# A decoder trunk in float32r: h as contiguous rows of 512 values at one byte offset from the weights

## The chip, the cores and the metric

The kernel runs on one core of one Trainium2 chip. The metric is the device time of one execution in microseconds (us). The time before is 2643.68 us, the median of three runs (2642.72 to 2644.52).

The engines are named as in the profile: PE is TensorE (matmuls), PEld its weight loads, DVE VectorE, ACT ScalarE, POOL GpSimd, SP SyncE. SBUF is the on-chip memory with 128 partitions, PSUM the memory of eight banks that matmuls write. A matmul holds a block of 128 x 128 weights, the stationary operand, which a weight load puts in place beforehand, and streams the moving operand past it, up to 512 values per partition. Offsets in this text are bytes within a partition.

## The reference, cut to what matters

The reference is a trunk of two layers for one sequence of 256 tokens with a width of 2048. Layer 0 has a retention mixer of eight heads, layer 1 a short gated convolution. Each is followed by a SwiGLU feed-forward part with an inner width of 5632. Ahead of each of these four parts stands a normalization with a shift and a scale that come from a conditioning vector c:

```python
for i in range(DEPTH):
    mod = (c_act @ w_mod[i] + b_mod[i])[:, None, :]
    sh1, sc1, g1, sh2, sc2, g2 = jnp.split(mod, 6, axis=-1)
    h = (rms_norm(x, norm1_g[i]) * (1.0 + sc1) + sh1).astype(x.dtype)
    ...
    x = (x + g1 * y).astype(x.dtype)
    h = (rms_norm(x, norm2_g[i]) * (1.0 + sc2) + sh2).astype(x.dtype)
    x = (x + g2 * swiglu(h, ffn_w_in[i], ffn_w_out[i])).astype(x.dtype)
return rms_norm(x, final_g).astype(x.dtype)
```

Most of the work lies in the products of activations with float32 weight matrices: `ret_w_in`, `ret_w_out`, `ffn_w_in` and `ffn_w_out` (twice), `conv_w_in` and `conv_w_out`. In the retention mixer q and k are rotated by `rope`:

```python
t1, t2 = t[..., :half], t[..., half:]
return jnp.concatenate([t1 * cos - t2 * sin, t2 * cos + t1 * sin], axis=-1)
```

## The kernel before, in words

**Layout.** The model width lies on the partitions: x and every activation are kept as 16 tiles (index j or k) of 128 rows by 256 tokens. A product with a weight matrix goes over k, and for each k over the columns of a group of weight columns (class `Group`).

**Two halves.** The matmuls take the type float32r, which holds fewer bits than float32. So every number is split in a high half, the value rounded to float32r, and a low half, the remainder. A product of two split numbers is made of three parts: high by high, high weights by low activations, low weights by high activations. An activation tile has the shape [128, 2, 256], high half first.

**Weights.** All weights lie in one array in the order of use. `fetch` loads chunks of 128 x 2048 float32 by DMA from SP's queue. `prepare` (from L297) splits half a chunk, 1024 columns, into a tile hi (ScalarE, L312) and a tile lo (VectorE, L315). The pool `wpool` has four tiles each of hi and lo, of 4096 bytes per partition. `take` (L320) hands out the next 128 columns of hi and lo, so blocks of weights stand 512 bytes apart in these tiles.

**Products.** There are four ways, all on TensorE, whose order is as written in the program:

- `product` (from L347) makes a pair of matmuls for each block: L357 streams all 512 values of the activation tile, both halves, past the high weights; L360 streams the 256 values of the high half past the low weights.
- `packed` (from L376) makes three matmuls of 256 values, L397 to L399, which add up in 256 columns of a bank.
- `by_token` (from L367) makes the values of the retention. It holds blocks of h (128 tokens of one half) as weights and streams hi and lo, 512 columns each: L372 to L374, once for each half of the tokens.
- `normed` (from L493) makes the first columns of the stage behind a normalization: six columns (`LEAD`), while the root of the norm is still unknown. h is then only x times its scale (`scaled_only`, L484). For every k all the columns of the group follow one another (L516 to L518). The row of h has two tokens more than 256 here: the shift, split in a high and a low part, so that the product with the shift comes out in columns of its own. `total` (L529) multiplies the sum by the root and adds the product with the shift (`end`).

**Activation operands.** These are `h_all` in the pool `hpool` (L481), 16 tiles with two halves of 256 + 2 values each, so that the halves of one tile stand 258 values apart; `rm` tiles (from L567), the retention's middle; and `mid` tiles (from L939), the middle of the feed-forward part and of the convolution. rm and mid tiles are contiguous rows of 512 values. The pools are declared in the order `const`, `work`, `wpool`, `hpool`, then `rm` and `rpool`, or `mpool` after these are closed.

**Order of stages.** The retention's input goes first: four spans over some heads and some k, then head by head in a fixed order (`projections`, L915), with the first half of its output product (`ret_out`) after four heads and the second after eight. The feed-forward part runs in two halves of 22 tiles, each followed by its output product. The convolution follows, and the second feed-forward part. `rope` (L804) rotates q and k of a head on VectorE: one product of 512 values with the cosine, two of 256 with the sine, and two of 256 to add them up. Its input lies in PSUM, or, for heads whose product was begun in the spans, in an SBUF tile (`pair`, L899). Between the products the modulations of the next stages are made (`modulation`, L241), as VectorE products with the spread vector c; `paced` (L269) says when.

Of the kernel before, what the change touches and what calls it, by code (L numbers as in the profile page):

```python
# [10 lines left out]
F32 = mybir.dt.float32  # L11
F32R = mybir.dt.float32r
I32 = mybir.dt.int32
AF = mybir.ActivationFunctionType
ALU = mybir.AluOpType
PSUM = bass.MemoryType.PSUM

P = 128
D = 2048
S = 256  # L20
KT = D // P
# [27 lines left out]
STEPS = (8, 8, 20)  # L49
RAW_BUFS = 3  # L50
PART_BUFS = 4

Q0, K0, V0, G0 = 0, HEADS * DK, 2 * HEADS * DK, 2 * HEADS * DK + HEADS * DV
SH1, SC1, GT1, SH2, SC2, GT2 = range(6)
# [133 lines left out]
def trunk(ctx: ExitStack, tc: tile.TileContext, x_in, c_in, pos_in, w_mod, cols_in, tab_in, w_all, out):  # L188
    nc = tc.nc
    const = ctx.enter_context(tc.tile_pool(name="const", bufs=1))  # L190
    work = ctx.enter_context(tc.tile_pool(name="work", bufs=2))
    wpool = ctx.enter_context(tc.tile_pool(name="wpool", bufs=PART_BUFS))
    ps = ctx.enter_context(tc.tile_pool(name="ps", bufs=8, space=PSUM))
# [3 lines left out]
    def name(s):  # L197
        serial[0] += 1
        return f"{s}_{serial[0]}"

    def tmp(tag, shape=(P, S), dtype=F32, pool=work, bufs=None):
        return pool.tile(list(shape), dtype, tag=tag, name=name(tag), bufs=bufs)
# [30 lines left out]
    mod_s = [[const.tile([P, KT], F32, tag=f"s{l}{i}", name=f"s{l}{i}") for i in range(2)] for l in range(DEPTH)]  # L233
# [35 lines left out]
    def paced(n):  # L269

        units[0] += n
        due = 0
        for (a, i), (b, j) in zip(plan_mod, plan_mod[1:]):
            if units[0] >= a:
                due = min(j, i + (units[0] - a) * (j - i) // (b - a))
        allowed[0] = min(allowed[0] + n * MOST, 2.0) if n <= 64 else 0.0
        while todo and n_mod - len(todo) < due and allowed[0] >= 1.0:
            allowed[0] -= 1.0
            modulation(*todo.pop())

    def needed(layer, which, last=KT - 1):
        while any(m[:2] == (layer, which) and m[2] <= last for m in todo):
            modulation(*todo.pop())
# [36 lines left out]
    def take(group, k, col, width=P):  # L320

        assert order.pop() == (group, k, col, width)
        i = taken_cols[0] % HALF
        if i == 0:
            if ready and taken_cols[0]:
                ready.pop(0)
            while len(ready) < 1 + AHEAD * (units[0] >= first):
                n = len(ready)
                prepare()
                if len(ready) == n:  # L330
                    break
        taken_cols[0] += width
        return [t[:, i : i + width] for t in ready[0]]

    def bank():
        return ps.tile([P, 2, S], F32, tag="bank", name=name("bank"))
# [91 lines left out]
    def norm_sums(accs):  # L428

        pt = bank()  # L430
        for t in range(2):
            for i, acc in enumerate(accs):
                nc.tensor.matmul(
                    pt[:, 0, t : t + 1], acc[:, t * P : (t + 1) * P], ones[:, 0:1],
                    start=i == 0, stop=i == len(accs) - 1,
                )
        return pt

    def norm_roots(pt, n):
        return roots_of(pt[:, 0, 0:2], n)  # L440
# [9 lines left out]
    def norm_spread(r):  # L450

        pb = bank()
        for t in range(2):
            nc.tensor.matmul(
                pb[:, 0, t * P : (t + 1) * P], r[:, t : t + 1].to_broadcast([P, P]), ident, start=True, stop=True
            )
        return pb[:, 0, :]
# [18 lines left out]
    def modulated(h, j, rb, layer, norm):  # L476
        shifted(h, scaled(j, rb, layer, norm), j, layer, norm)

    hpool = ctx.enter_context(tc.tile_pool(name="hpool", bufs=1))

    h_all = hpool.tile([P, KT, 2, S + 2], F32R, tag="h", name="h")  # L481
    h = [h_all[:, j, :, :S] for j in range(KT)]

    def scaled_only(layer, norm, j):  # L484

# [7 lines left out]
    def normed(accs, layer, norm, g):  # L493

        needed(layer, SH2 if norm else SH1)
        shift = mod_s[layer][norm].unsqueeze(2).to_broadcast([P, KT, 2])  # L500
        ends = [h_all[:, :, i, S:] for i in range(2)]
        nc.scalar.copy(ends[0], shift)
        nc.vector.tensor_tensor(ends[1], shift, ends[0].bitcast(F32), op=ALU.subtract)
        banks = [bank().rearrange("p a b -> p (a b)")[:, : S + 2] for _ in g.cols]
        made = [0]

        def more(n):
            while made[0] < n:
                modulated(h[made[0]], made[0], root, layer, norm)
                made[0] += 1  # L510

        for k in g.ks:
            rows = [h_all[:, k, i, :] for i in range(2)]
            for c, pt in zip(g.cols, banks):
                hi, lo = take(g, k, c)
                nc.tensor.matmul(pt, hi, rows[0], start=k == 0, stop=False)  # L516
                nc.tensor.matmul(pt, hi, rows[1], start=False, stop=False)  # L517
                nc.tensor.matmul(pt, lo, rows[0], start=False, stop=k == KT - 1)  # L518
            if k == ROOTS_AT:
                r = norm_roots(norm_sums(accs), D)  # L520
            elif k == SPREAD_AT:
                root = tmp("rb", bufs=1)
                nc.scalar.copy(root, norm_spread(r))
            elif k > SPREAD_AT:
                more(min(k, made[0] + 2))
        more(KT)
        paced(len(g.cols) * len(g.ks))

        def total(pt, dst=None):  # L529
            end = tmp("end", (P, 1), bufs=2)  # L530
            nc.scalar.copy(end, pt[:, S : S + 1])
            t = tmp("low", bufs=3)
            nc.vector.tensor_tensor(t, pt[:, :S], root, op=ALU.mult)
            dst = tmp("sum", bufs=4) if dst is None else dst
            nc.scalar.activation(dst, t, AF.Identity, bias=end)
            return dst

        return [lambda dst=None, pt=pt: total(pt, dst) for pt in banks]

    def output(groups, act, which, last, after=None, base=None):  # L540
# [25 lines left out]
    with ExitStack() as inner:  # L566
# [46 lines left out]
        sin = rm.tile([P, S], F32, tag="sin", name="sin")  # L613
        cos = rm.tile([P, S], F32, tag="cos", name="cos")
        ahead = {}
# [15 lines left out]
        with tc.tile_pool(name="start", bufs=1) as sp:  # L631
# [59 lines left out]
            with tc.manual_schedule(engines={mybir.EngineType.DVE, mybir.EngineType.Activation}):  # L691
# [16 lines left out]
                for i in range(0, D, 2 * S):  # L708
                    pt = bank().rearrange("p a b -> p (a b)")
# [24 lines left out]
                pt = norm_sums([acc[0][:, 0, :]])  # L734
# [66 lines left out]

        rp = inner.enter_context(tc.tile_pool(name="rpool", bufs=1))

        def rope(s, tag):  # L804
            a = tmp("qa", (P, 2, S), pool=rp, bufs=1)
            nc.vector.tensor_tensor(a, s, cos.unsqueeze(1).to_broadcast([P, 2, S]), op=ALU.mult)
            b = tmp("qb", (P, 2, S), pool=rp, bufs=1)
            nc.vector.tensor_tensor(b[:, 0, :], s[:, 1, :], sin, op=ALU.mult)
            nc.vector.tensor_tensor(b[:, 1, :], s[:, 0, :], sin, op=ALU.mult)
            nc.vector.tensor_tensor(a[:, 0, :], a[:, 0, :], b[:, 0, :], op=ALU.subtract)  # L810
            nc.vector.tensor_tensor(a[:, 1, :], a[:, 1, :], b[:, 1, :], op=ALU.add)
            dst = rp.tile([P, 2, 2, S], F32R, tag=tag, name=name(tag))
            nc.scalar.copy(dst[:, 0, :, :], a)
            nc.vector.tensor_tensor(dst[:, 1, :, :], a, dst[:, 0, :, :].bitcast(F32), op=ALU.subtract)
            return dst

        def gate(s):

            g = rp.tile([P, 2, S], F32, tag="sg", name=name("sg"), bufs=2)
            nc.scalar.activation(g, s, AF.Silu)  # L820
            return g.rearrange("p a b -> p (a b)")
# [77 lines left out]
        def pair(head, i):  # L899

            g = RET_HEADS[head][0][i]
            if not g.ks:
                return [ahead[head, n] for n in ((i,) if i < 2 else (2, 3))]
            sums = packed(g, h)
            for j, pt in enumerate(sums):
                key = (head, i + j)
                if key in tag_of:
                    free.append(tag_of.pop(key))
                if key in ahead:
                    s = tmp("qs", (P, 2, S), pool=rp, bufs=1)  # L910
                    nc.vector.tensor_tensor(s, ahead[key], pt, op=ALU.add)
                    sums[j] = s
            return sums

        def projections(head):  # L915
            q = rope(*pair(head, 0), "q")
            k = rope(*pair(head, 1), "k")
            v = values(head, RET_HEADS[head][1])
            sp = scores(head, q, k)
            sg = [gate(s) for s in pair(head, 2)]  # L920
            asides.extend(mixed(head, sp, v, sg))
            since[0] = 0
# [48 lines left out]
    for i, g in enumerate(CONV_IN):  # L971
        pending += [sums(g)] if i else normed(acc, 1, 0, g)
        while len(pending) >= 3:
            pb, pc, pu = pending[:3]
            pending = pending[3:]
            j = done
            b, c, u = pb(tmp("bsum", pool=mpool, bufs=2)), pc(), pu()
# [73 lines left out]
```

## Time and profile before

| what | value |
|---|---|
| median of the three runs | 2643.68 us |
| the profiled execution, its own time | 2641.89 us |
| its span, from the first to the last instruction | 2640.1 us |
| mean granted TensorE clock | 0.998 |
| matmuls on PE | 15220 |
| bytes read from HBM | 682.99 MB, 259 GB/s over the span |

Pairs (L357 and L360) run in long chains, by operand and stage: with rm in windows such as 374.8 to 429.9 us and 715.7 to 774.7 us; with h such as 1169.8 to 1399.7 us; with mid such as 1402.8 to 1514.8 us.

How to read the rows that follow: a group has its line in the kernel, the engine, the operation, output <- inputs by the names of the tiles, the shape, and the count (x3296); behind the first bar stand the busy time in us and the mean of one in ns, behind the second the idle time of the engine ahead of them and what ended it. A row of a single line's view has the least, median and largest duration in ns, and the start of the first and of the last instruction in us. A row of the timeline has the start and the duration in us. Matmuls are pipelined and their ends are modelled, so durations of neighbours overlap; their starts are recorded.

### The profile page before, as it was taken

The numbers are of one execution on the slowest core, as the hardware profiler recorded it, in microseconds if no ns is written. First come the engines' busy times: TensorE is split into PE (matmuls) and PEld (weight loads), VectorE is DVE, ScalarE is ACT, GpSimd is POOL, SyncE is SP. The second block draws the span as 40 slices with busy tenths as digits, with TensorE's granted clock in tenths as the row PEclk, the third lists the DMA queues.
The fourth block names the chain that finished last, engine by engine and source line by source line (L and its number), as shares of the span: only waits on it lengthen the run. The fifth ranks groups of instructions, "written<-read, shape, count | busy, mean of one in ns | idle before, by whom it ended". The sixth has DMA issues, their size and how long they took to land.

```text
span 2640.1 us, 38225 instructions
## 1 busy us (share of the span) xinstructions
PE 2608.1 (99%) x15220; PEld 2291.2 (87%) x15220; DVE 1990.3 (75%) x2543; ACT 1244.8 (47%) x1770; POOL 146.6 (6%) x230
## 2 busy tenths in 40 slices
PE   7999999999999999999999999999999999999998
PEld 5888889888889888888888898888988888888887
DVE  7998878777698877777777888888886765555554
ACT  5644443444455444344444454444554443444443
POOL 0000001010000011110100001100000000000000
PEclk9999999999999999999999999999999999999999
DMA  9976668776686877777777768777677655555553
GB/s 397 391 273 256 258 242 317 258 271 259 251 300 243 314 283 272 273 283 283 287 270 282 268 224 321 280 281 262 253 277 263 248 219 191 190 191 187 183 190 127
DMA packets 96950, 687.58 MB, mean 260 GB/s; under 512 B 10753, under 2 KB 12545, under 8 KB 13825
## 3 DMA queue, kind: packets, MB, share of 16 engines
q1 hardware_dynamic: 96770, 685.13, 70.0%
q8 instruction: 119, 1.95, 0.3%
q14 instruction: 61, 0.50, 0.1%
HBM read 682.99 MB, written 2.10 MB: 259 GB/s over the span
## 4 chain that ended last, share of the span: by engine, by line
PE 76%; issue 19%; DVE 2%; DMA 1%; ACT 1%; POOL 0%; DVEq 0%; POOLq 0%; ACTq 0%
PE bank L357 35%; PE bank L360 18%; PE bank L372 4%; PE bank L373 4%; PE bank L374 4%; PE bank L399 2%; PE bank L398 2%; PE bank L397 2%; PE bank L517 1%; PE bank L516 1%; PE bank L518 1%; DVE raw L642 1%; DMA raw<-w_all 1%; PE bank L869 1%; DVE lo L315 1%
## 5 line engine op out<-in xcount | busy, mean ns | idle before, releaser
L315 DVE TENSOR_TENSOR lo<-raw,hi 128x1024 fp32r<-128x1024 f32 x912 | 1111.5, 1222 | 551.6 <-ACT hi L312 549.3
L312 ACT CAST hi<-raw 128x1024 fp32r<-128x1024 f32 x912 | 953.2, 1050 | 1088.9 <-PE bank L357 649.0
L357 PE MATMUL bank<-h,hi 128*128 128x512 f32 x3296 | 1155.2, 395 | 0.0
L360 PE MATMUL bank<-h,lo 128*128 128x256 f32 x3296 | 924.4, 280 | 0.0
L357 PEld LDWEIGHTS bank<-h,hi 128*128 128x128 f32 x3296 | 622.6, 189 | 145.3
L360 PEld LDWEIGHTS bank<-h,lo 128*128 128x128 f32 x3296 | 622.0, 189 | 0.0
L357 PE MATMUL bank<-mid,hi 128*128 128x512 f32 x1604 | 556.3, 393 | 0.0
L360 PE MATMUL bank<-mid,lo 128*128 128x256 f32 x1604 | 444.9, 277 | 0.6 <-DVE lo L315 0.6
L246 DVE SCALAR_TENSOR_TENSOR raw<-raw,cb 128x2048 f32<-128x2048 f32 x160 | 365.4, 2284 | 11.7 <-DMA raw<-w_mod 11.3
L357 PEld LDWEIGHTS bank<-mid,hi 128*128 128x128 f32 x1604 | 300.7, 187 | 69.4
L360 PEld LDWEIGHTS bank<-mid,lo 128*128 128x128 f32 x1604 | 301.3, 188 | 0.9 <-DVE lo L315 0.9
L372 PE MATMUL bank<-hi,h 128*128 128x512 f32 x512 | 202.7, 396 | 0.0
L373 PE MATMUL bank<-lo,h 128*128 128x512 f32 x512 | 201.9, 394 | 0.0
L374 PE MATMUL bank<-hi,h 128*128 128x512 f32 x512 | 201.9, 394 | 0.0
L357 PE MATMUL bank<-rm,hi 128*128 128x512 f32 x496 | 174.2, 396 | 0.0
L399 PE MATMUL bank<-h,lo 128*128 128x256 f32 x512 | 145.6, 284 | 9.1 <-DVE lo L315 9.1
L397 PE MATMUL bank<-h,hi 128*128 128x256 f32 x512 | 144.9, 283 | 2.5 <-ACT h L670 2.5
L398 PE MATMUL bank<-h,hi 128*128 128x256 f32 x512 | 144.8, 283 | 0.5 <-DVE h L671 0.5
L360 PE MATMUL bank<-rm,lo 128*128 128x256 f32 x496 | 138.5, 279 | 0.0
L374 PEld LDWEIGHTS bank<-hi,h 128*128 128x128 f32 x512 | 96.3, 188 | 22.7
L372 PEld LDWEIGHTS bank<-hi,h 128*128 128x128 f32 x512 | 96.6, 189 | 19.6
L373 PEld LDWEIGHTS bank<-lo,h 128*128 128x128 f32 x512 | 96.4, 188 | 19.6
(152 smaller groups left out, 2239.3 us busy)
## 6 DMA issues: line engine op xcount, KB each, us to landing
raw<-w_all SPq DMA_DIRECT2D x456, 1024.0 KB, 4.8
raw<-w_mod SPq DMA_DIRECT2D x192, 1024.0 KB, 5.0
x<-x_in SPq DMA_DIRECT2D x4, 512.0 KB, 5.7
out<-out SPq DMA_DIRECT2D x5, 256.0 KB, 3.4
decay<-tab_in SPq DMA_DIRECT2D x8, 128.0 KB, 2.2
out<-out SPq DMA_DIRECT2D x3, 128.0 KB, 2.5
out<-out SPq DMA_DIRECT2D x1, 384.0 KB, 2.7
cols<-cols_in SPq DMA_DIRECT2D x1, 160.0 KB, 8.8
```

What stands on the lines that cost most here:

```text
L246: nc.vector.scalar_tensor_tensor(raw, raw, 1.0, cb, op0=ALU.mult, op1=ALU.mult, accum_out=total)
L312: nc.scalar.copy(hi, raw)
L315: nc.vector.tensor_tensor(lo, raw, hi.bitcast(F32), op=ALU.subtract)
L357: nc.tensor.matmul(pt, hi, h, start=fresh and k == g.ks[0], stop=False, skip_group_check=True)
L360: nc.tensor.matmul(pt[:, 1, :], lo, h[:, 0, :], start=False, stop=last and k == g.ks[-1], skip_group_check=True)
L372: nc.tensor.matmul(o, ht[:, 0, :], hi, start=first, stop=False)
L373: nc.tensor.matmul(o, ht[:, 0, :], lo, start=False, stop=False)
L374: nc.tensor.matmul(o, ht[:, 1, :], hi, start=False, stop=last)
L397: nc.tensor.matmul(pt, hi, h[:, 0, :], start=first, stop=False, skip_group_check=True)
L398: nc.tensor.matmul(pt, hi, h[:, 1, :], start=False, stop=False, skip_group_check=True)
L399: nc.tensor.matmul(pt, lo, h[:, 0, :], start=False, stop=last, skip_group_check=True)
L516: nc.tensor.matmul(pt, hi, rows[0], start=k == 0, stop=False)
```

## The change

The change has three parts.

1. h's row becomes 32 values of margin and then the two halves, 256 values each, side by side: [128, 16, 32 + 512] in place of [128, 16, 2, 258]. A tile of 8 values (32 bytes per partition) that nothing uses is taken ahead of h_all in the same pool.
2. The shift's two tokens, its high and its low part, stand in the last two values of the margin, in front of the high half. In `normed` the high rows keep 258 values (two tokens and 256), the low rows have 256 and are added to columns 2 and on of the bank. Before, the high half's tokens held the shift's high part and the low half's its low part, so one column of the bank had the whole product; now its two parts come out in two columns, and `total` adds them with one small ScalarE instruction more.
3. `rope` makes both sine products in one instruction of 512 values, written over its input where that lies in SBUF (`ours`), and else to a tile under the tag qs. The tile qb is gone.

Order, groups, loads and the number of matmuls stay.

```diff
+LEFT, MARGIN = 8, 32
...
-    h_all = hpool.tile([P, KT, 2, S + 2], F32R, tag="h", name="h")
-    h = [h_all[:, j, :, :S] for j in range(KT)]
+    hpool.tile([P, LEFT], F32, tag="aside", name="aside")
+    h_all = hpool.tile([P, KT, MARGIN + 2 * S], F32R, tag="h", name="h")
+    h = [h_all[:, j, MARGIN:].rearrange("p (a b) -> p a b", a=2) for j in range(KT)]
...
-        shift = mod_s[layer][norm].unsqueeze(2).to_broadcast([P, KT, 2])
-        ends = [h_all[:, :, i, S:] for i in range(2)]
+        shift = mod_s[layer][norm].unsqueeze(2)
+        ends = [h_all[:, :, MARGIN - 2 + i : MARGIN - 1 + i] for i in range(2)]
...
-            rows = [h_all[:, k, i, :] for i in range(2)]
+            high, low = h_all[:, k, MARGIN - 2 : MARGIN + S], h[k][:, 1, :]
...
-                nc.tensor.matmul(pt, hi, rows[0], start=k == 0, stop=False)
-                nc.tensor.matmul(pt, hi, rows[1], start=False, stop=False)
-                nc.tensor.matmul(pt, lo, rows[0], start=False, stop=k == KT - 1)
+                nc.tensor.matmul(pt, hi, high, start=k == 0, stop=False, skip_group_check=True)
+                nc.tensor.matmul(pt[:, 2:], hi, low, start=False, stop=False, skip_group_check=True)
+                nc.tensor.matmul(pt, lo, high, start=False, stop=k == KT - 1, skip_group_check=True)
...
-            end = tmp("end", (P, 1), bufs=2)
-            nc.scalar.copy(end, pt[:, S : S + 1])
+            low_end = tmp("end", (P, 1), bufs=4)
+            nc.scalar.copy(low_end, pt[:, 1:2])
+            end = tmp("end", (P, 1), bufs=4)
+            nc.scalar.activation(end, pt[:, 0:1], AF.Identity, bias=low_end)
             t = tmp("low", bufs=3)
-            nc.vector.tensor_tensor(t, pt[:, :S], root, op=ALU.mult)
+            nc.vector.tensor_tensor(t, pt[:, 2:], root, op=ALU.mult)
...
-        def rope(s, tag):
+        def rope(s, tag, ours):
+
             a = tmp("qa", (P, 2, S), pool=rp, bufs=1)
             nc.vector.tensor_tensor(a, s, cos.unsqueeze(1).to_broadcast([P, 2, S]), op=ALU.mult)
-            b = tmp("qb", (P, 2, S), pool=rp, bufs=1)
-            nc.vector.tensor_tensor(b[:, 0, :], s[:, 1, :], sin, op=ALU.mult)
-            nc.vector.tensor_tensor(b[:, 1, :], s[:, 0, :], sin, op=ALU.mult)
-            nc.vector.tensor_tensor(a[:, 0, :], a[:, 0, :], b[:, 0, :], op=ALU.subtract)
-            nc.vector.tensor_tensor(a[:, 1, :], a[:, 1, :], b[:, 1, :], op=ALU.add)
+            b = s if ours else tmp("qs", (P, 2, S), pool=rp, bufs=1)
+            nc.vector.tensor_tensor(b, s, sin.unsqueeze(1).to_broadcast([P, 2, S]), op=ALU.mult)
+            nc.vector.tensor_tensor(a[:, 0, :], a[:, 0, :], b[:, 1, :], op=ALU.subtract)
+            nc.vector.tensor_tensor(a[:, 1, :], a[:, 1, :], b[:, 0, :], op=ALU.add)
...
-            q = rope(*pair(head, 0), "q")
-            k = rope(*pair(head, 1), "k")
+            q = rope(*pair(head, 0), "q", (head, 0) in ahead)
+            k = rope(*pair(head, 1), "k", (head, 1) in ahead)
```

## The prediction

> **What bounds the kernel now.** I read the first two parts of the page first, then the chain of waits.
>
> ```profile
> span 2640.1 us, 38225 instructions
> PE 2608.1 (99%) x15220; PEld 2291.2 (87%) x15220; DVE 1990.3 (75%) x2543; ACT 1244.8 (47%) x1770; POOL 146.6 (6%) x230
> ...
> PEclk9999999999999999999999999999999999999999
> ...
> PE 76%; issue 19%; DVE 2%; DMA 1%; ACT 1%; POOL 0%; DVEq 0%; POOLq 0%; ACTq 0%
> PE bank L357 35%; PE bank L360 18%; PE bank L372 4%; PE bank L373 4%; PE bank L374 4%; PE bank L399 2%; PE bank L398 2%; PE bank L397 2%; PE bank L517 1%; PE bank L516 1%; PE bank L518 1%; DVE raw L642 1%; DMA raw<-w_all 1%; PE bank L869 1%; DVE lo L315 1%
> ```
>
> TensorE is the bound: it is busy 99% of the span at the full granted clock, and the chain runs through its matmuls and their issue. So the time changes by what the pitch of the matmuls changes, that is the time from the start of one to the start of the next. The groups say how many there are of each kind:
>
> ```profile
> L357 PE MATMUL bank<-h,hi 128*128 128x512 f32 x3296 | 1155.2, 395 | 0.0
> L357 PE MATMUL bank<-mid,hi 128*128 128x512 f32 x1604 | 556.3, 393 | 0.0
> L372 PE MATMUL bank<-hi,h 128*128 128x512 f32 x512 | 202.7, 396 | 0.0
> L357 PE MATMUL bank<-rm,hi 128*128 128x512 f32 x496 | 174.2, 396 | 0.0
> ```
>
> Each L357 (512 values) is followed by one L360 (256 values); I call the two a pair. The mean of one (395 ns) is no pitch, as ends are modelled and overlap. For the pitch I took the view of line L357 alone in four windows that hold nothing but pairs, one row for each (count, durations, first and last start):
>
> ```profile
> L357 PE MATMUL bank<-h,hi x657: 389/396/400, 1169.8 to 1399.7; 128*128 128x512 f32 x165
> L357 PE MATMUL bank<-mid,hi x324: 392/394/395, 1402.8 to 1514.8; 128*128 128x512 f32 x162
> L357 PE MATMUL bank<-rm,hi x160: 392/394/395, 374.8 to 429.9; 128*128 128x512 f32 x160
> L357 PE MATMUL bank<-rm,hi x168: 395/398/403, 715.7 to 774.7; 128*128 128x512 f32 x168
> ```
>
> First to last start over the count less one: **h 229.9 / 656 = 350.5 ns a pair**, mid 112.0 / 323 = 346.7, rm 55.1 / 159 = 346.5 in the first half and 59.0 / 167 = 353.3 in the second. The four windows run the same instructions on the same shapes with no wait, and differ by 2%.
>
> **Where the rows lie.** If tiles lie one behind another in the order of the pools, every weight block starts at a multiple of 512 bytes within hi and lo (4096 bytes each), and h follows them. A row of h has 2 x 258 x 4 = 2064 bytes, 16 more than a multiple of 128, so h[k] starts 16k bytes off the weights: the offset steps through eight values as k runs. mid and rm tiles have 2048 bytes; all start at the same offset, and as 16 x 2064 is a multiple of 128 that offset is 0. So before, h sweeps and mid and rm hold 0. One sweep, in the timeline of TensorE (first rows of the pairs k = 0 to 3, 6, 7, 10, 11, and k = 0 of the next column):
>
> ```profile
> 1295.63 0.39 PE L357 MATMUL bank<-h,hi 128*128 128x512 f32 x1
> ...
> 1295.97 0.39 PE L357 MATMUL bank<-h,hi 128*128 128x512 f32 x1
> ...
> 1296.32 0.39 PE L357 MATMUL bank<-h,hi 128*128 128x512 f32 x1
> ...
> 1296.67 0.39 PE L357 MATMUL bank<-h,hi 128*128 128x512 f32 x1
> ...
> 1297.71 0.40 PE L357 MATMUL bank<-h,hi 128*128 128x512 f32 x1
> ...
> 1298.07 0.40 PE L357 MATMUL bank<-h,hi 128*128 128x512 f32 x1
> ...
> 1299.13 0.40 PE L357 MATMUL bank<-h,hi 128*128 128x512 f32 x1
> ...
> 1299.48 0.40 PE L357 MATMUL bank<-h,hi 128*128 128x512 f32 x1
> ...
> 1301.23 0.39 PE L357 MATMUL bank<-h,hi 128*128 128x512 f32 x1
> ```
>
> The pair takes 0.34 us at k = 0 and 0.36 at k = 6; the cycle of 16 takes 5.60, 350 ns a pair. The pitch does depend on the row.
>
> **The change part by part.** *Held offset.* With MARGIN a row of h has 544 x 4 = 2176 bytes, 17 x 128, and the 32-byte tile in front puts every row of h 32 bytes past a multiple of 128 from the weights; the rows behind h move along, since 16 x 2176 is a multiple of 128. So every chain will hold one offset, 32. What does a held offset cost? Three chains that hold one:
>
> ```profile
> 303.54 0.85 PE L869 MATMUL bank<-v,sp 128*128 128x512 f32 x3
> 304.22 0.28 PE L397 MATMUL bank<-h,hi 128*128 128x256 f32 x1
> ...
> 1518.70 0.28 PE L397 MATMUL bank<-mid,hi 128*128 128x256 f32 x1
> ...
> 1520.86 0.28 PE L397 MATMUL bank<-mid,hi 128*128 128x256 f32 x1
> ...
> 789.98 0.28 PE L516 MATMUL bank<-h,hi 128*128 128x258 f32 x1
> ...
> 791.42 0.28 PE L516 MATMUL bank<-h,hi 128*128 128x258 f32 x1
> ```
>
> Three matmuls of 512 at offset 0: 0.68 / 3 = 226.7 ns each. Eighteen of 256 at offset 0: 2.16 / 18 = 120.0 ns. The last two rows lie in the normed product, which stays at one k for all its columns; this is k = 2, offset 32 (low half 40), and four triples of 258 take 1.44, that is 120.0 ns a matmul. From the first two: (226.7 - 120.0) / 256 = 0.417 ns a value, and 13.3 ns a matmul on top. (16 values, 64 bytes, take 6.7 ns, and 6.7 is also what parts the two rm windows: I call it a step.) A pair then costs 768 x 0.417 + 2 x 13.3 = 346.7 ns, which is what mid takes. The held chain at 32 fits the same law (258 values: 120.9).
>
> So my value for h is 346.7, by the row it becomes most like: one contiguous row of 512 with a held offset, as mid. 3296 x (346.7 - 350.5) = **-12.5 us**. The bounds are 340 (the cheapest pair of the sweep, k = 0) and 353.3 (the dear rm window, and about what the sweep pays at k = 2, 6, 10: 0.35, 0.36, 0.35): -34.6 and +9.2 us.
>
> *mid and rm* go from held 0 to held 32: mid stays at 346.7, **0**, with bounds 340 and 353.3: -10.7 and +10.6 us (1604 pairs). The dear half of rm, 248 pairs, settles at the law: 248 x -6.6 = **-1.6 us**; bounds -3.3 and 0. The cheap half moves as mid would: 0, bounds -1.6 and +1.7.
>
> *Values by token* (L372 to L374) stream the weights past blocks of h, so they sweep too, and have not the law's 226.7:
>
> ```profile
> 290.26 0.39 PE L372 MATMUL bank<-hi,h 128*128 128x512 f32 x1
> ...
> 298.62 0.39 PE L372 MATMUL bank<-hi,h 128*128 128x512 f32 x1
> ```
>
> Twelve triples in 8.36: 232.2 ns. Held, 1536 x (226.7 - 232.2) = **-8.4 us**; bounds -18 (220, one step of 6.7 lower) and 0 (the sweep as it is).
>
> *Packed products on h* (L397 to L399) stand at about 120 already; 0, bounds +-2 us (1536 matmuls by the 1 ns that a timeline of 0.01 us does not resolve). *The shift's tokens in front* leave the high row at 258 and cut the low one to 256: 288 x 2 x 0.417 = -0.24 us.
>
> *Other engines.* rope does one sine product of 512 instead of two of 256, and total one more ScalarE copy of a column:
>
> ```profile
> L806 DVE TENSOR_TENSOR qa<-qs,cos 128x512 f32<-128x512 f32 x8 | 5.5, 683 | 0.1
> L808 DVE TENSOR_TENSOR qb<-qs,sin 128x256 f32<-128x256 f32 x8 | 3.3, 416 | 0.0
> L531 ACT COPY end<-bank 128x1 f32<-128x1 f32 x18 | 2.2, 147 | 0.0
> ```
>
> 16 x (2 x 416 - 683) = 2.4 us less on VectorE, 18 x 0.147 = 2.6 us more on ScalarE. Both lie under TensorE's pairs, and I cost them at nothing. The copies come six or five to a stage, 0.9 us, while two of the eight banks stay free for further columns of 16 pairs (5.6 us each). Without that cover it would be +2.6 us; the VectorE saving can be worth at most its 2.4. No DMA and no queue is moved.
>
> **Sum**: -12.5 - 1.6 - 8.4 - 0.2 = -22.7 us. The profiled execution took 2641.89 us, 1.8 below the median of 2643.68 and 0.8 below the lowest of the three, so a median run would come out that much higher: **2619 us** from the profiled one, 2621 from the median. I say 2620, 0.9% faster.
>
> **The rivals.** *Fewer stalls* (faster still). If 32 bytes keep weight loads and rows apart, each pair falls one step of 6.7 ns below mid's, to 340: -34.6 - 10.7 - 3.3 - 1.6 and the tokens' -8.4 give -58.6, 2583 us. For it: the sweep holds a pair of 340, so the law is no floor, and other offsets than 0 have never been held in long chains. Against: the one chain held at 32 shows 120.0, no less than at 0.
>
> *Dearer at 32* (slower). Row and weight block are read at the same time, and half a step's 64 bytes apart one may hold up the other twice instead of once; then all pairs lock at the 353.3 that rm shows: +9.2 + 10.6 + 1.7, tokens unchanged: +21.5, 2663 us. For it: in the sweep k = 2, 6, 10, all 32 off a multiple of 64, are dear. Against: there the offset has just moved, and what one pair pays may have been made by the pair before. It decides from a pair pitch of 350.9, where (with the tokens' gain) the 5396 pairs cost as much as now.
>
> *No dependence on place*, the time stays at 2642 (+-3). The sweep of 0.34 to 0.36 and the two rm windows speak against it. [...]
>
> *The front tile does not shift anything* (it is never read, and may be dropped): then all chains hold 0 and the forecast's sum stands as it is; it is no case of its own.
>
> **How the numbers follow.** Forecast 0.36, fewer stalls 0.24, dearer 0.32, no dependence 0.08. Faster by over 0.2% (5 us, about what a measurement of this kernel tells from no change): 0.60; within 0.2%: 0.08; slower: 0.32. The forecast's own range is 2610 to 2630, from tokens that gain nothing to tokens at 220. Cases of both signs hold much of the chance, so the range reaches to them: down to 2578, just under the fewer-stalls sum, up to 2664, just over the dearer one.
>
> **What would show it.** Right: the windows of h and mid both give 346.7 ns a pair with the same counts, the token triples fall from 697 to 680 ns, and the rm windows are alike. Wrong by place: h and mid together at 340 or at 353.3; by the held-offset step: h and mid apart, or an h pitch that still depends on k. A cover that fails would show TensorE idle before L357 or L360 right after a normed stage.

## The result and the profile after

The changed kernel takes 2639.5 us (median of 22 runs, 2637.41 to 2643.2), the kernel before 2643.94 us (22 runs beside them, 2641.26 to 2646.61). The ratio is 0.9985, 95% interval 0.9978 to 0.9992: 4.4 us faster, a gain that the interval tells from none, and a fifth of the 23 that were forecast.

The first parts of the page of the changed kernel, and the share of the span by engine in its chain of waits:

```profile
span 2637.7 us, 38238 instructions
PE 2604.2 (99%) x15220; PEld 2299.1 (87%) x15220; DVE 1989.0 (75%) x2527; ACT 1249.3 (47%) x1788; POOL 151.3 (6%) x230
...
PEclk9999999999999999999999999999999999999999
...
PE 75%; issue 20%; DVE 2%; DMA 2%; ACT 1%; POOL 0%; DVEq 0%; ACTq 0%; POOLq 0%
```

TensorE is still the bound, busy 99% of the span at a mean granted clock of 0.998, so the answer lies in the pitches again. The view of the one line that starts a pair, now L358 (L361 is its second half), in the same four windows of the changed kernel; the columns are count, durations in ns, first and last start in us:

```profile
L358 PE MATMUL bank<-h,hi x652: 389/392/402, 1169.9 to 1397.7; 128*128 128x512 f32 x163
L358 PE MATMUL bank<-mid,hi x319: 390/390/395, 1402.6 to 1512.9; 128*128 128x512 f32 x160
L358 PE MATMUL bank<-rm,hi x155: 389/390/391, 374.6 to 428.0; 128*128 128x512 f32 x155
L358 PE MATMUL bank<-rm,hi x162: 389/390/391, 715.9 to 771.7; 128*128 128x512 f32 x162
```

h takes 227.8 / 651 = **349.9 ns** a pair (before 350.5), mid 110.3 / 318 = 346.9, rm 53.4 / 154 = 346.8 and 55.8 / 161 = 346.6. mid stayed, rm's dear half came down as forecast, and h did not move. The timeline of TensorE in the changed kernel shows what its pairs do (first rows of pairs; between the fifth and the last lie 11 more):

```profile
1199.65 0.39 PE L358 MATMUL bank<-h,hi 128*128 128x512 f32 x1
1200.00 0.39 PE L358 MATMUL bank<-h,hi 128*128 128x512 f32 x1
1200.34 0.40 PE L358 MATMUL bank<-h,hi 128*128 128x512 f32 x1
1200.70 0.39 PE L358 MATMUL bank<-h,hi 128*128 128x512 f32 x1
1201.05 0.39 PE L358 MATMUL bank<-h,hi 128*128 128x512 f32 x1
...
1205.25 0.39 PE L358 MATMUL bank<-h,hi 128*128 128x512 f32 x1
```

The starts are 0.35, 0.34, 0.36, 0.35 apart, and this repeats every four pairs: 1.40 us for four, 5.60 for sixteen. (Taken to the nanosecond and averaged over the window, the four steps are 348, 348, 359 and 345 ns.) mid, whose rows by their sizes all lie at one offset, shows no such period: its four steps in the window above, taken the same way, are 346 to 347 ns. Rows 2176 bytes apart advance by 128 modulo 512, so they come back to the same place every four rows. That suggested where to look.

The values by token did not fall from 697 to 680 ns a triple either. Timeline of L373, changed kernel, first and last of ten triples:

```profile
292.85 0.39 PE L373 MATMUL bank<-hi,h 128*128 128x512 f32 x1
...
299.15 0.40 PE L373 MATMUL bank<-hi,h 128*128 128x512 f32 x1
```

Nine steps in 6.30 us are 700 ns a triple, 233.3 a matmul, 1.1 more than before. Two small gains that were not forecast are in the timeline of the products of 256 and 258 values, packed on mid (L398) and normed (L519), 20 and 10 triples of three matmuls apart:

```profile
1516.70 0.28 PE L398 MATMUL bank<-mid,hi 128*128 128x256 f32 x1
...
1523.70 0.28 PE L398 MATMUL bank<-mid,hi 128*128 128x256 f32 x1
```

```profile
786.03 0.28 PE L519 MATMUL bank<-h,hi 128*128 128x258 f32 x1
...
789.58 0.28 PE L519 MATMUL bank<-h,hi 128*128 128x258 f32 x1
```

A packed matmul takes 7.00 / 60 = 116.7 ns, before 120.0; a normed triple 355, before 360.

**Where the time came from**, by these rows: h 3296 x (349.9 - 350.5) = -2.0 us; rm's second half 248 x (346.6 - 353.3) = -1.7; tokens 1536 x 1.1 = +1.7; normed 288 x -5 ns = -1.4; packed on mid 60 x -10 ns = -0.6. The sum, -4.0 us, lies near the 4.4 us of the medians, but it does not account for the time in full. The rows come from two executions that lie 2.4 us apart (2641.89 and 2639.47), and the list leaves out two items of that size: the packed products on h, which went from 357.2 to 353.3 ns a triple where they follow one another (512 triples, about -2.0 us), and pauses between matmuls, about 3 us more than before. Both come from the starts of the matmuls in the two traces.

### The profile page after: what moved, and what is told of

The parts are those of the page before. It is cut to its first block, busy times and chain, and to the rows that moved or that the text cites. A ratio compares the mean times of both kernels' runs of the same rounds, so it can differ in the third digit from the quotient of the medians.

```text
span 2637.7 us, 38238 instructions
## 1 busy us (share of the span) xinstructions
PE 2604.2 (99%) x15220; PEld 2299.1 (87%) x15220; DVE 1989.0 (75%) x2527; ACT 1249.3 (47%) x1788; POOL 151.3 (6%) x230
## 4 chain that ended last, share of the span: by engine, by line
PE 75%; issue 20%; DVE 2%; DMA 2%; ACT 1%; POOL 0%; DVEq 0%; ACTq 0%; POOLq 0%
PE bank L358 34%; PE bank L361 18%; PE bank L374 4%; PE bank L375 4%; PE bank L373 4%; PE bank L400 2%; PE bank L398 2%; PE bank L399 2%; PE bank L519 1%; PE bank L521 1%; PE bank L520 1%; DMA raw<-w_mod 1%; DVE raw L647 1%; DMA raw<-w_all 1%; DVE lo L316 1%
## 5 line engine op out<-in xcount | busy, mean ns | idle before, releaser
L358 PE MATMUL bank<-h,hi 128*128 128x512 f32 x3296 | 1153.8, 394 | 0.0
L361 PE MATMUL bank<-h,lo 128*128 128x256 f32 x3296 | 926.4, 281 | 0.0
L358 PEld LDWEIGHTS bank<-h,hi 128*128 128x128 f32 x3296 | 617.9, 187 | 140.0
L361 PEld LDWEIGHTS bank<-h,lo 128*128 128x128 f32 x3296 | 624.5, 189 | 0.0
L358 PE MATMUL bank<-mid,hi 128*128 128x512 f32 x1604 | 556.3, 390 | 0.0
L361 PE MATMUL bank<-mid,lo 128*128 128x256 f32 x1604 | 452.5, 282 | 1.1 <-DVE lo L316 1.1
L358 PEld LDWEIGHTS bank<-mid,hi 128*128 128x128 f32 x1604 | 301.1, 188 | 63.0
L361 PEld LDWEIGHTS bank<-mid,lo 128*128 128x128 f32 x1604 | 303.4, 189 | 1.5 <-DVE lo L316 1.5
L374 PE MATMUL bank<-lo,h 128*128 128x512 f32 x512 | 203.3, 397 | 0.2 <-DVE lo L316 0.2
L373 PE MATMUL bank<-hi,h 128*128 128x512 f32 x512 | 203.4, 397 | 0.0
L358 PE MATMUL bank<-rm,hi 128*128 128x512 f32 x496 | 172.5, 391 | 0.0
L398 PE MATMUL bank<-h,hi 128*128 128x256 f32 x512 | 144.7, 283 | 2.5 <-ACT h L675 2.5
L361 PE MATMUL bank<-rm,lo 128*128 128x256 f32 x496 | 139.9, 282 | 0.0
L375 PEld LDWEIGHTS bank<-hi,h 128*128 128x128 f32 x512 | 96.6, 189 | 23.3
L374 PEld LDWEIGHTS bank<-lo,h 128*128 128x128 f32 x512 | 96.5, 189 | 20.7 <-DVE lo L316 0.6
L373 PEld LDWEIGHTS bank<-hi,h 128*128 128x128 f32 x512 | 96.6, 189 | 20.2
```

What stands on the lines that cost most here:

```text
L358: nc.tensor.matmul(pt, hi, h, start=fresh and k == g.ks[0], stop=False, skip_group_check=True)
L361: nc.tensor.matmul(pt[:, 1, :], lo, h[:, 0, :], start=False, stop=last and k == g.ks[-1], skip_group_check=True)
L373: nc.tensor.matmul(o, ht[:, 0, :], hi, start=first, stop=False)
L374: nc.tensor.matmul(o, ht[:, 0, :], lo, start=False, stop=False)
L375: nc.tensor.matmul(o, ht[:, 1, :], hi, start=False, stop=last)
L398: nc.tensor.matmul(pt, hi, h[:, 0, :], start=first, stop=False, skip_group_check=True)
```

## The experiments

Three theories for h's 350 ns stood at the start. A: the offset between row and weight block counts modulo 512, not 128, and a chain pays when it moves. B: the same, but of the row alone. C: something else in h, not its stride. Every kernel below is an edit of the changed kernel unless said otherwise, and the kernel before, run beside them, had medians of 2643.97 to 2644.76 us. Offsets are worked out from the order and the sizes of the tiles, as in the prediction; no run shows an address.

**Rows 2560 bytes apart**, five times 512. The wider margin takes room, so hi has three buffers instead of four, `low` two instead of three, and one tile moves to another pool. A second kernel has only these smaller buffers, with rows at 2176.

```diff
-LEFT, MARGIN = 8, 32
+LEFT, MARGIN = 8, 128
...
-        hi = wpool.tile([P, HALF], F32R, tag="hi", name=name("hi"))
+        hi = wpool.tile([P, HALF], F32R, tag="hi", name=name("hi"), bufs=3)
...
-            t = tmp("low", bufs=3)
+            t = tmp("low", bufs=2)
```

> Base: the changed kernel (2639.5 us; pairs on h 350.0 ns with one pair in four about 11 ns dearer, on mid and rm 346.7). Here h's rows stand 2560 bytes apart (a margin of 128 values), a multiple of 512, in place of 2176; room comes from three hi tiles and two low tiles and one shared root tile. Theory A (row against weights: a pair is dear when the offset between row and weight block changes modulo 512 from pair to pair) and theory B (row against row: it is dear when a row starts elsewhere modulo 512 than the row before): h 346.7 ns a pair, 3296 x 3.3 = 11 us less; the token triples fall from 233 to 227 a matmul if the held law holds there, 10 us more; 2618 to 2629 us. Theory C (the place of the rows does not count, h has another reason): h stays at 350.0, 2639 us.

> The control for the run with the margin of 128: only its fewer buffers (three hi, two low, a shared root tile), rows 2176 bytes apart as in the changed kernel. All theories: the changed kernel's time, 2639 us, and h at 350.0 ns a pair; if one tile fewer makes TensorE wait, some us more, and idle time before L358 or L361 shows it.

The line of the pairs on h, first with rows 2560 apart, then with the smaller buffers alone:

```profile
L358 PE MATMUL bank<-h,hi x664: 390/390/390, 2260.0 to 2489.8; 128*128 128x512 f32 x166
```

```profile
L358 PE MATMUL bank<-h,hi x630: 390/392/401, 1179.8 to 1399.9; 128*128 128x512 f32 x158
```

With 2560, 229.8 / 663 = 346.6 ns, and the durations are 390 in least, median and largest: no pair stands out as dearer. With 2176, 220.1 / 629 = 349.9. The times: 2642.33 us (ratio to the kernel before 0.9998, 0.9989 to 1.0007) against 2652.12 (a single run). The 9.8 us between them answer to 3296 x 3.3 ns = 10.9, within what single runs scatter (the eleven with 2560 lie between 2638.62 and 2647.96). So the forecast's price of a held pair was right; the rows at 2176 do not hold. The 2618 to 2629 us expected by A and B were missed, mainly because the smaller buffers cost 12.6 us next to the change (2639.5), more than the stride brings. The waits of TensorE, with the smaller buffers and then in the changed kernel (us in all, times, longest):

```profile
PE bank L361 <- DVE lo L316: 4.6, 5, 1.2
```

```profile
PE bank L361 <- DVE lo L316: 1.1, 1, 1.1
```

These two rows show 3.5 us of that. The rest is in pauses too: the pitches are those of the change, but summed from start to start over the whole trace the kernel with the smaller buffers spends 6.5 us more than the change on the pairs on h, 1.9 on rm's, 2.1 on the values by token and 1.6 on the packed products on mid.

The tokens tell a second thing. L373 in the kernel with rows 2560 apart, two starts that are ten triples apart:

```profile
294.78 0.40 PE L373 MATMUL bank<-hi,h 128*128 128x512 f32 x1
...
301.78 0.40 PE L373 MATMUL bank<-hi,h 128*128 128x512 f32 x1
```

7.00 / 30 = 233.3 ns, the same as in the change. So at 32 bytes holding does not bring them to 226.7.

**mid at h's stride.** mid tiles get the same 2176 bytes, of which 2048 are used.

```diff
+    def mid_tile(i):
+        t = mpool.tile([P, MARGIN + 2 * S], F32R, tag=f"mid{i}", name=name("mid"))
+        return t[:, : 2 * S].rearrange("p (a b) -> p a b", a=2)
```

> The changed kernel with the mid tiles 2176 bytes apart in place of 2048, their rows of 512 still contiguous. Theories A and B: mid rises from 346.7 to 350.0 ns a pair, 1604 x 3.3 = 5.3 us more, 2645 us; rm stays. Theory C: mid stays at 346.7, 2639 us.

The line of the pairs on mid in this kernel:

```profile
L358 PE MATMUL bank<-mid,hi x309: 390/392/401, 1404.9 to 1512.7; 128*128 128x512 f32 x155
```

107.8 / 308 = 350.0 ns, from 346.7, with the durations that h shows at this stride (390/392/401). So the stride alone took contiguous rows of 512 from 346.7 to 350.0; C falls. The time of a single run was 2645.01 us.

**Weight blocks 640 bytes apart.** Now the weights advance by 128 modulo 512 from block to block, as h's rows do, while mid's rows stay 2048 apart. A and B part here: by A h becomes cheap and mid dear, by B nothing changes.

```diff
-        hi = wpool.tile([P, HALF], F32R, tag="hi", name=name("hi"))
+        hi = wpool.tile([P, HALF // P, P + PAD], F32R, tag="hi", name=name("hi"), bufs=3)
...
-        return [t[:, i : i + width] for t in ready[0]]
+            return [t[:, i // P, :P] for t in ready[0]]
```

> The changed kernel with blocks of weights 640 bytes apart in place of 512 (three tiles of hi and of lo). Rows of h (2176 apart) now advance against the blocks by 1536, a multiple of 512; rows of mid and rm (2048 apart) by 128 off one. Theory A: h falls to 346.7 ns a pair and mid and rm rise to 350.0. Theory B: h stays at 350.0 and mid and rm at 346.7. Theory C: no pitch moves. The time by A is 11 us less on h and 7 more on mid and rm, 2635; by B and C 2639; waits for one buffer fewer come on top.

The line of the pairs in this kernel (here L361):

```profile
L361 PE MATMUL bank<-h,hi x630: 390/394/397, 1179.7 to 1399.9; 128*128 128x512 f32 x158
...
L361 PE MATMUL bank<-mid,hi x301: 392/396/396, 1414.9 to 1519.9; 128*128 128x512 f32 x151
```

h stays at 220.2 / 629 = 350.1, against A; mid rises to 105.0 / 300 = 350.0, against B. Both fall. What is left, as a bare finding: in the kernels with the 32 bytes so far pairs took 349.9 to 350.1 ns where either stream, rows or weight blocks, advanced by 128 modulo 512 at every step, against 346.6 to 346.9 where neither did, and moving both together did not make up for it (350.1 on h here). The trace also has a period of two here and not of four: starts to the nanosecond step by 354 and 346 ns on h, 348 and 352 on mid. That would fit a modulus of 256 bytes for the weights, an estimate from these steps alone; no run moves either stream by 256. The time was 2659.62 us (a single run), with the buffers of hi and lo down to three.

**Smaller margins**: rows 2112 and 2080 bytes apart, advancing by 64 and by 32.

```diff
-LEFT, MARGIN = 8, 32
+LEFT, MARGIN = 8, 16
```

> The changed kernel with a margin of 16 values: rows of h 2112 bytes apart, an advance of 64 per row where the changed kernel has 128; mid and rm stay at 32. If each change of place costs the same: h at 350.0 ns a pair. If it costs by its distance (13.3 ns per 512 bytes): 2 units of 6.7 ns in 8 rows, 348.3. If places by themselves count (the offsets 32 and 96 in turn): between 346.7 and 350.2, which 32 and 96 bytes showed when held.

> The changed kernel with a margin of 8 values: rows of h 2080 bytes apart, an advance of 32 per row, so the offset runs through 0, 32, 64 and 96 modulo 128; mid and rm stay at 32. If each change of place costs the same: 350.0 ns a pair. If it costs by its distance: 2 units in 16 rows, 347.5. If places by themselves count: the mean of 353.3, 346.7, 353.3 and 350.2, which is 350.9.

Two windows of the first kernel, then one of the second (MARGIN = 8):

```profile
L358 PE MATMUL bank<-h,hi x615: 391/397/398, 1179.8 to 1394.7; 128*128 128x512 f32 x154
...
L358 PE MATMUL bank<-h,hi x570: 394/396/398, 1579.8 to 1779.9; 128*128 128x512 f32 x190
```

```profile
L358 PE MATMUL bank<-h,hi x614: 392/395/399, 1179.8 to 1394.9; 128*128 128x512 f32 x154
```

Advancing by 64, one chain takes 214.9 / 614 = 350.0 ns and another, same instructions, 200.1 / 569 = 351.7; by 32 it takes 215.1 / 613 = 350.9. The price did not grow with the advance: 32, 64 and 128 all cost 3.3 to 5.0 ns a pair over 346.7. A law that prices a move by its distance misses these (348.3 and 347.5 were its values). One that prices the places met the 350.9, and of the two chains with 64 the 350.0 but not the 351.7; one price for every move met only the 350.0. Single runs took 2643.43 and 2644.78 us.

**Rows in another order.** This keeps every buffer. Row k lies in slot 4(k mod 4) + k div 4, so three of four steps go 4 x 2176 = 8704 = 17 x 512 bytes, and only four in sixteen advance by 128.

```diff
+SLOT = [4 * (k % 4) + k // 4 for k in range(KT)]
...
-    h = [h_all[:, j, MARGIN:].rearrange("p (a b) -> p a b", a=2) for j in range(KT)]
+    h = [h_all[:, SLOT[j], MARGIN:].rearrange("p (a b) -> p a b", a=2) for j in range(KT)]
```

It ran with the change's 32 bytes in front, and with 0, 64 and 96.

> The changed kernel with h's rows put in memory in another order (slot 4 * (k mod 4) + k div 4), so that rows used one after the other stand 8704 bytes apart, a multiple of 512, but for one step in four; no buffer is given up. Theory D, which the runs so far leave (what costs is an advance of rows or of weight blocks that is no multiple of 512, whichever of the two it is): 16 rows go once around 512 bytes instead of four times, so the 13.3 ns that four pairs pay now are paid by 16: h at 347.5 ns a pair, 3296 x 2.5 = 8 us less than the changed kernel, 2631 us. Rival (the sum of distances counts, or each step to another place costs the same whatever its size): four steps in 16 off the multiple, a quarter of the extra: also 347.5; if the size of the step counts (here +128 too): the same. Rival E (the gain of the run with 2560 came from its buffers): 350.0 and 2639 us.

> As the run with the slots, without the 32-byte tile: rows start at a multiple of 128 from the weights. If the 32 bytes buy anything once the rows hold their place: mid, rm and h dearer than 346.7 to 347.5, most likely with windows at 353.3 as in the kernel before (rm second half): up to 5396 x 6.7 = 36 us more than with 32. If they buy nothing but the choice between such states: 346.7 in most windows, within 5 us of the run with 32. Values by token: 227 a matmul if the held law of the three v rows is right at offset 0, 8 us less than at 32; 233 if not.

> As the run with the slots, with a tile of 64 bytes: rows start 64 bytes past a multiple of 128. If the offset counts modulo 64 (16 values take one step of 6.7 ns): the same pitches as without the tile. If modulo 128: pitches of its own, between 340 and 353.3 ns a pair.

> As the run with the slots, with a tile of 96 bytes. If the offset counts modulo 64: the same pitches as with 32 bytes, 346.7 on mid and 347.5 on h, 2631 us. If modulo 128: pitches of its own, between 340 and 353.3 ns a pair.

The line of the pairs (here L359), on h and on mid, with 32 bytes in front:

```profile
L359 PE MATMUL bank<-h,hi x618: 390/392/397, 1179.9 to 1394.8; 128*128 128x512 f32 x155
...
L359 PE MATMUL bank<-mid,hi x301: 390/390/390, 1405.9 to 1509.9; 128*128 128x512 f32 x151
```

The same with 0, with 64 and with 96 bytes (mid):

```profile
L359 PE MATMUL bank<-mid,hi x293: 395/398/403, 1406.6 to 1509.8; 128*128 128x512 f32 x147
```

```profile
L359 PE MATMUL bank<-mid,hi x294: 392/397/398, 1406.1 to 1509.7; 128*128 128x512 f32 x147
```

```profile
L359 PE MATMUL bank<-mid,hi x286: 392/393/394, 2149.9 to 2249.7; 128*128 128x512 f32 x143
```

| bytes in front | us | mid, ns a pair | h, ns a pair |
|---|---|---|---|
| 32 | 2633.69 | 346.7 | 348.3 |
| 0 | 2654.89 | 353.3 | 351.7 |
| 64 | 2655.82 | 353.3 | 352.5 |
| 96 | 2655.83 | 350.0 | 350.9 |

(The pitches are from starts to the nanosecond; the rows above, with starts to 0.1 us, give the same within 0.3 ns.)

With 32 this is the fastest kernel of all: ratio 0.9966 to the kernel before (0.9952 to 0.998). h's pairs fell by 1.7 ns to 348.3 and not to the held 346.7: four steps in sixteen still advance, at about 6.7 ns each on average (4 x 6.7 / 16 = 1.7). The theories of what a move costs had put 347.5 ahead of the run, half that price, so none of them has it right. 3296 x -1.7 = -5.6 us answers to the 5.8 between this kernel and the change. The other three are single runs. mid's own tiles are the same in all four; only their offset to the weights differs, and 32 is the best of the four offsets tried. 96 is not as 32 (350.0 against 346.7 on mid), so the offset does not count modulo 64 here.

**Without the 32 bytes**, nothing else changed:

```diff
-    hpool.tile([P, LEFT], F32, tag="aside", name="aside")
```

> The changed kernel without the 32-byte tile: rows of h still 2176 apart, rows of every kind start at a multiple of 128 from the weights. Theory two-state (at offset 0 a chain of pairs can lock at 346.7 or at 353.3 ns and keeps what it fell into; at 32 only 346.7 is found): mid and rm chains stand at 346.7 or 353.3 each, mostly 353.3 if the contiguous rows of h lead there, as with the slots: 2640 to 2660 us. Rival (offset 0 was dear only with the slots' order): mid at 346.7 throughout, h at 350, 2640 us or a little under, as tokens run at 230 instead of 233.

Four windows of one execution of this kernel, the last two from one chain:

```profile
L358 PE MATMUL bank<-mid,hi x312: 395/398/403, 1039.9 to 1149.8; 128*128 128x512 f32 x156
...
L358 PE MATMUL bank<-mid,hi x301: 391/391/391, 1405.9 to 1509.9; 128*128 128x512 f32 x151
...
L358 PE MATMUL bank<-mid,hi x67: 393/398/403, 1796.4 to 1819.7; 128*128 128x512 f32 x67
...
L358 PE MATMUL bank<-mid,hi x88: 391/391/391, 1839.7 to 1869.8; 128*128 128x512 f32 x88
```

At offset 0 a chain of this kernel ran at 109.9 / 311 = 353.4 ns or at 104.0 / 300 = 346.7, kept to it over these hundreds of pairs, and in one case changed over midway (23.3 / 66 = 353.0, then 30.1 / 87 = 346.0). The two rm windows of the kernel before showed the same two pitches, with rows at 0 modulo 128, though at 256 modulo 512. Which one a chain takes seems fixed by the program and not by chance: here both first halves of the feed-forward parts run at 353.4 and both second halves at 346.7, and the kernel with rope alone (below), whose rows and weights lie as in the kernel before, has the dear pitch in the same rm window (718.8 to 777.8 us, 59.0 / 167 = 353.3). h went the other way, to 348.3:

```profile
L358 PE MATMUL bank<-h,hi x618: 390/393/393, 1179.9 to 1394.8; 128*128 128x512 f32 x155
```

The time is 2639.81 us, ratio 0.9982 (0.9972 to 0.9991), the same as the change. So in this layout the 32 bytes buy nothing on balance: they keep mid at 346.7, where without them some chains run at 353.4, and cost h 1.7 ns a pair, 5.6 us. By the starts of the whole trace they also cost the values by token about 4 us (699.9 ns a triple against 691.8) and save about 3 on the packed and normed products: the kinds of matmul do not agree on one best offset. Nor does holding always help: without the bytes, the reordered rows gave h 351.7, dearer than the 348.3 of rows that move.

**rope alone**, the change's third part put into the kernel before:

```diff
-            nc.vector.tensor_tensor(b[:, 0, :], s[:, 1, :], sin, op=ALU.mult)
-            nc.vector.tensor_tensor(b[:, 1, :], s[:, 0, :], sin, op=ALU.mult)
+            nc.vector.tensor_tensor(b, s, sin.unsqueeze(1).to_broadcast([P, 2, S]), op=ALU.mult)
```

> The kernel before with rope's new form alone (one sine product of 512 values, in place where it can be). All theories: TensorE's pairs hide it, 2644 us and a ratio of 1.000 within 0.002; VectorE busy 2.4 us less. Rival (the VectorE path counts): up to 2.4 us less.

The time is 2644.68 us, ratio 1.0003 (0.9994 to 1.0013). The group shows that the work is shorter, 686 ns for one product of 512 where two of 256 took 2 x 416; no gain shows in the time:

```profile
L809 DVE TENSOR_TENSOR qs<-qs,sin 128x512 f32<-128x512 f32 x8 | 5.5, 686 | 0.1
```

## Why the prediction was wrong, and where it was right

- **The step that failed is "Held offset"**: that with rows 17 x 128 bytes apart "every chain will hold one offset, 32". Modulo 128 they do, but that is not enough. The period of four in the changed kernel, mid at 350.0 with h's stride, and h at 346.6 with rows 2560 apart show it: the rows that held advance by multiples of 512 (2048, 2560, and 8704 in the reordered kernel), those that advance by 128, 64 or 32 did not. The modulus of 128 was a choice, as mid's 2048 bytes are a multiple of 512 as well, and the trace of before spoke against it. There h[k] and h[k + 8] lie at the same offset modulo 128, so the sweep should repeat every eight rows; but starts to the nanosecond, averaged over the window of h, give 341.7 ns for the pair at k = 0 and 347.5 for the one at k = 8. Both signs of failure that the prediction names for this step came: h and mid stand apart, and h's pitch still depends on k. The term of -12.5 us measured about -2.0.
- **The price of a held pair was right**: 346.7 ns forecast, 346.6 measured with 2560. At that stride most of the -12.5 is there: 9.8 us between the two kernels with smaller buffers.
- **Values by token failed as well**, with another cause: a price found at offset 0 was carried to 32. The forecast took 226.7 ns from three matmuls on v at offset 0. Fully held at offset 32, the tokens take 233.3. L374 in the kernel with reordered rows and no bytes in front, three starts, seven triples and then three apart:

```profile
294.44 0.40 PE L374 MATMUL bank<-hi,h 128*128 128x512 f32 x1
...
299.33 0.39 PE L374 MATMUL bank<-hi,h 128*128 128x512 f32 x1
...
301.37 0.39 PE L374 MATMUL bank<-hi,h 128*128 128x512 f32 x1
```

  The first seven triples take 4.89 / 21 = 232.9 ns a matmul, the last three 2.04 / 9 = 226.7. The last three belong to k = 12 on, whose rows start at multiples of 512 bytes in this layout; through this run the rows of k = 4 to 7, at 256 bytes, take the same 680 ns a triple, and the others, 128 bytes off these places, about 698. So the 226.7 is real, for held rows at such a place, and was not to be had at 32. The term of -8.4 became +1.7. Why these matmuls, whose weights are rows of h and whose stream is the weight matrix, go by other places than pairs stays open.
- **mid, rm**: right. mid stayed at 346.7 to 346.9 and rm's dear half settled, -1.7 us for a forecast -1.6.
- **Packed and normed products**: costed at nothing and -0.24; those on mid and the normed ones gave about -2 us (120.0 to 116.7 ns, 360 to 355 a triple) and those on h about as much. The law of 0.417 ns a value and 13.3 ns a matmul was drawn from rows at offset 0 and does not carry over to 32: there 256 values take 116.7 where it has 120.0, and 512 take 233.3 where it has 226.7.
- **rope and the copies**: hidden, as forecast. The added copies and sums in the changed kernel:

```profile
L536 ACT ACTIVATE end<-bank,end 128x1 f32<-128x1 f32 x18 | 4.6, 257 | 0.4
...
L534 ACT COPY end<-bank 128x1 f32<-128x1 f32 x18 | 2.7, 150 | 0.1
```

  The addition is an ACTIVATE of 257 ns, so it is 4.6 us on ScalarE and not the 2.6 that I took from the copy; TensorE shows no wait for it.
- **The rivals.** "Dearer at 32" came true only in part, through h (350.0 against 348.3 without the bytes) and the tokens, far from a lock at 353.3. "Fewer stalls" did not occur: no held chain went under 346.0, and none to 340. "No dependence on place" came nearest in time (2642) and is wrong as a mechanism: the same instructions on the same buffers took 346.6 ns a pair with rows 2560 bytes apart and 349.9 with rows 2176 apart. That weight loads and rows hold each other up, from which the first two rivals argue, was the author's estimate and is not shown: the traces show that the two overlap (in the changed kernel PE is busy 2604.2 and PEld 2299.1 of 2637.7 us) and what a pair takes.

Left open: why an advance of either stream costs, whether an advance of 256 bytes would be as cheap as one of 512, what picks the pitch at offset 0, and why tokens differ. Not tried: offsets in steps below 32 bytes, and a stride that is a multiple of 512 with all buffers kept, such as 2048 bytes with the shift's two tokens elsewhere.

## What to carry to other kernels

Where TensorE runs without waits, take the pitch from first and last starts of a chain; here chains of the same instructions differed by up to 2% (346.5 to 353.4 ns a pair), and other strides of the rows alone moved h by 1% (349.9 with 2176 bytes, 346.6 with 2560). It paid, by 0.3% of the time before (2633.69 us, ratio 0.9966), to let rows and weight blocks advance by multiples of 512 bytes as often as the order of the rows allows, with rows 32 bytes off the weights, and it didn't pay to give up buffers for it (12.6 us in a single run). When a layout is said to hold something, compute it in every modulus that the chain taken as the model satisfies, not in the smallest that fits, and look in the trace for the period that each of them would give. A price that was measured at one offset need not hold at another: here 512 values took 226.7 ns in rows at offset 0 and 233.3 by token at 32.

## What the runs showed of the hardware

All of this is what the traces of these runs show; offsets and advances are worked out from the sizes and the order of the tiles.

- In the long chains of these runs the pitch of a pair of float32r matmuls (512 and 256 values, a weight load each) lay between 346.5 ns (rm, the kernel before) and 353.4 (mid, the changed kernel without the 32 bytes), at a granted clock of 0.996 to 0.998.
- At offset 0 modulo 128 two pitches stood beside each other, in the kernel before (rm, 346.5 and 353.3) and in the changed kernel without the 32 bytes (mid, 346.7 and 353.4), where a chain kept to one over 301 and 312 pairs. At 32 bytes long chains whose rows repeat modulo 512 showed only 346.6 to 346.9. In the reordered kernels mid showed 353.3 at 64 bytes and 350.0 at 96.
- With rows 32 bytes off, an advance of 128 bytes modulo 512 cost 3.3 ns a pair when every pair made it (349.9 against 346.6 on h), and about 6.7 ns each on average when four in sixteen did (348.3 on h); rows alone and weight blocks alone cost the same (350.0 on mid). Without the 32 bytes, h's rows made the same advance at 348.3.
- Matmuls of 512 values with a row of h as weights took 233.3 ns with rows 32 bytes off, and in the reordered kernel without these bytes 226.7 where rows that hold their place start at multiples of 256 bytes.
